# A hybrid attention step on one core: mixer B's transposes moved between the high and low parts of mixer A's values

## The chip, the cores and the metric

The kernel runs on one core of a Trainium2 chip. The metric is the device time of one execution, in microseconds (us). A core has five engines that run side by side, each through its own instructions in order: TensorE (PE; its weight loads are shown apart, as PEld), VectorE (DVE), ScalarE (ACT), GpSimd (POOL) and SyncE (SP, which here issues most of the DMA transfers). A product on TensorE has a stationary operand (the weights, loaded before the pass) and a moving one that streams past it; results land in PSUM, a memory of eight banks, from which the other engines read.

## The reference

One step of a diffusion backbone for 1024 latent tokens and 128 prompt tokens of width 1024, all in float32. A modulated RMSNorm is projected into queries, keys, values and gates of two mixers with 8 heads and 2 key heads each; both mixers attend, are gated, and are projected out together. Cut to what matters here:

```python
p = h @ w_in
q_a, k_a, v_a, g_a, q_b, k_b, v_b, g_b = split(p)     # keys and queries are normalised, turned by position
# mixer A: softmax over 128 context keys and all 1024 latent keys
s = einsum(q_a, k_all) * d ** -0.5 ;  o_a = einsum(softmax(s), v_all)
# mixer B: softmax over a sink column, 128 context keys and a band of 3 x 128 latent keys
s = concat([sink, s_ctx, s_band]) ;   o_b = einsum(softmax(s)[1:], v)
y = x + gate * (concat([o_a * silu(g_a), o_b * silu(g_b)]) @ w_out)
```

The prompt tokens attend to themselves alone, in both mixers.

## The kernel before

**Precision.** TensorE multiplies in a reduced float32 format. To reach the wanted accuracy, operands are split into a high and a low part, and a product becomes three: high by high, high by low, low by high.

**Stages.** First come the projections, up to about 304 us; the rest is attention with the output projection woven in. The attention is cut into *units* (t, m, g): a block t of 128 tokens, a mixer m (0 is A, 1 is B) and a key head g with its four query heads. The order is t = 1 to 8, g, m, so that A and B alternate, and four units of the prompt (t = 0) come last. A unit is cut into blocks of 128 keys, one for each *slot*: 9 slots for a unit of A, 4 for one of B (3 for t = 1 and t = 8), and for a prompt unit one with an empty one behind it. A pair of an A and a B unit so has 13 slots, or 12.

**A slot** is written out by the loop at the end of `hybrid_step`, and the order in which it issues work is kept on every engine (`in_order`). It goes through these steps:

- `tick()` runs what was put on an agenda with `later(n, f)`, n slots before.
- `scores()` of this slot's block. For mixer A: two products give the scores in a PSUM bank (L1190, and L1191 with the queries' low part and the negated row maximum as further rows, tile qb); ScalarE takes the exponential (L1193) and the high part ph (L1194); GpSimd, or VectorE for one block, the low part pl (L1198, L1196). For mixer B: the weights already exist (penat, tile pen), queries by keys, and four 128 x 128 transposes (L1185) turn a block; ScalarE copies the high part ph (L1186), VectorE takes the low part pl one slot later (L1187).
- what is `due` in this slot: row maxima of the A unit to come, and the scores of the B unit to come.
- products of the output projection (L1279), from a queue at OUTRATE in each slot, with the remainder carried over.
- `values()` of the block three slots back (LAG = 3): high values by ph (L1208), for mixer A also low values by ph (L1210, v_lo, 64 columns), high values by pl (L1211). All blocks of a unit add up in one bank.

**Row maxima** (`max_items`): an A unit has twelve, each a product of 384 columns (L918, pmx) and a reduction on VectorE (L919). MX_AT gives their slots, counted from the start of the A unit before (negative ones lie in the pair before that). At MX_END the second copy of the queries is loaded by SP's queue, and VectorE takes the maximum over them (m_nat); TURN slots later TensorE turns it (L937, ptm) and VectorE writes it into qb (L938).

**Mixer B's weights** (`weight_items`): in the first four slots of the A unit before it, a pair of products per head gives scores (L975, L976, tile sn); VectorE masks them and takes the row maximum (L979), ScalarE the exponential one slot later (L965). Then the sinks: a sum on GpSimd, the exponential on ScalarE (EX_AT[0] slots later), the total on GpSimd (EX_AT[1]), the reciprocal on VectorE (L1014, EX_AT[2]). The reciprocals are turned by TensorE (L1027, pti), copied by ScalarE (L1031) and go through DRAM to become rows, which multiply the gate. A prompt unit takes another way: one row maximum over all heads (L991), and VectorE scales the weights themselves (L1017).

**The end of a unit**, in slots counted from its last block by END_AT (PROMPT_END for the prompt): the inverse of the sums on ScalarE (L1222, L1223), the gating (two instructions on VectorE, L1232, and one on GpSimd, L1234), the split into parts, and the products for the output projection put on the queue.

**Banks.** Row maxima, sn, ptm and pti share two banks (A); scores and B's transposes two (B); values two (C); the projection's sums one each (D, E).

Of the kernel before, what the change touches and what calls it, by code (L numbers as in the profile page):

```python
# [9 lines left out]
F32 = mybir.dt.float32  # L10
# [3 lines left out]
ALU = mybir.AluOpType  # L14
# [4 lines left out]
P = 128  # L19
# [17 lines left out]
LAG = 3  # L37
# [4 lines left out]

NAT_AT = (0, 1, 2, 3)
NAT_FIRST = (0, 1, 2, 3)
MX_AT = (-4, -3, -2, -2, -1, 4, 5, 5, 7, 7, 8, 8)
MX_FIRST = (0, 1, 2, 3, 4, 4, 5, 5, 6, 7, 7, 8)
MX_END = 10
SPLIT_LAG = 2

LATE = (5, 5, 5, 5, 4)  # L50
# [3 lines left out]
WO_LATE = {12: 9, 13: 10, 11: 21, 15: 23, 14: 24}  # L54

WO_STEPS = ((0, 4, 4), (1, 5, 5), (2, 6), (3, 7), (4, 8, 6), (5, 9), (6, 11), (7, 12, 10), (8, 12), (9, 13), (10, 14))
TURN = 2
QUERY_AT = (0, 2, 3, 6)
PAD = 2
X_FROM = 2  # L60
# [7 lines left out]
BEHIND = ((), (), (), (), (0,), (1, 2), (3,), (4, 5), (6,), (7,))  # L68
WIDE = 5
LOADLEAD = 5  # L70
OUTRATE = 2.5
PADRATE = 3
POOL_LO = ("gb",)
NOG = 5
PES = 3
GATE_LATE = 2
END_AT = (1, 4, 6, 9)
PROMPT_END = (2, 4, 5, 7)
QTS = 5
PROMPT_LEAD = 4  # L80
EX_AT = (2, 2, 5)
ROWS_AT = (1, 1, 4, 6)
KV_ORDER = [0] + list(range(1, NT))
GATE_AT = (3, 7)
# [33 lines left out]
def hybrid_step(ctx, tc, x_prompt, x_sample, cache_k_a, cache_v_a, cache_k_b, cache_v_b,  # L118
# [3 lines left out]
    nc = tc.nc  # L122
# [13 lines left out]
    def later(n, f):  # L136

        agenda.setdefault(now[0] + n, []).append(f)
# [26 lines left out]
    ident_r = cst.tile([P, P], F32R, name="ident_r")  # L165
# [724 lines left out]
    penat = {}  # L890
# [10 lines left out]
    def max_items(i):  # L901
# [42 lines left out]
                out.append(lambda h=h, b=b: item(h, b))  # L944
        return out, finish

    def weight_items(i):

        t, m, g = units[i]
        v = {}  # L950

        def small(name):
            return qs.tile([P, 4], F32, tag=name, name=f"{name}{i}")

        def first(n):
            if t:
                penat[i] = qp2[0].tile([P, 4, 512], F32, tag="pen", name=f"pen{i}")[:, :, 0:n]
            else:
                penat[i] = w3.tile([P, 512], F32, tag="pe", name=f"pen{i}", bufs=PES).rearrange(
                    "p (h n) -> p h n", h=4)  # L960
            for x in ("nm", "sum", "ex", "inv"):
                v[x] = small(x)

        def exp(h, s, scale):
            nc.scalar.activation(penat[i][:, h], s, AF.Exp, bias=v["nm"][:, h : h + 1], scale=scale,  # L965
                                 accum_out=v["sum"][:, h : h + 1])

        def item(h):
            p0, p1_ = window(t)
            n = P * (p1_ - p0)  # L970
            if h == 0:
                first(n)
            lhs = qtile[i][:, P * h : P * h + P]
            s = bank("A", f"sn{i}_{h}")[:, 0:n]
            nc.tensor.matmul(s, lhs, khb[:, g, p0:p1_, :], start=True, stop=False)  # L975
            nc.tensor.matmul(s, lhs, klb[:, g, p0:p1_, :], start=False, stop=True)  # L976
            m0 = P if t == 1 else 0

            nc.vector.tensor_tensor_reduce(s, s, mask[:, m0 : m0 + n], -1.0, nsink[:, 4 * g + h : 4 * g + h + 1],  # L979
                                           op0=ALU.add, op1=ALU.min, accum_out=v["nm"][:, h : h + 1])  # L980
            later(1, lambda: exp(h, s, -1.0))

        def prompt():
            first(P)
            s = bank("A", f"sn{i}")
            for h in range(4):
                hs = slice(P * h, P * h + P)
                nc.tensor.matmul(s[:, hs], qtile[i][:, hs], khp[:, 2 + g, :], start=True, stop=False)
                nc.tensor.matmul(s[:, hs], qtile[i][:, hs], klp[:, 2 + g, :], start=False, stop=True)
            mx = small("mx4")  # L990
            nc.vector.tensor_reduce(mx, s.rearrange("p (h n) -> p h n", h=4), axis=AX.X, op=ALU.max)  # L991
            nc.vector.scalar_tensor_tensor(v["nm"], mx, -1.0, nsink[:, 4 * g : 4 * g + 4], op0=ALU.mult, op1=ALU.min)
            for h in range(4):
                exp(h, s[:, P * h : P * h + P], 1.0)

        def finish():
            nc.gpsimd.tensor_tensor(v["ex"], v["nm"], sink[:, 4 * g : 4 * g + 4], op=ALU.add)
            if t:
                later(EX_AT[0], sinks)
                later(EX_AT[1], total)  # L1000
                later(EX_AT[2], divide)
            else:
                sinks()
                later(1, total)
                later(1, divide)

        def sinks():
            nc.scalar.activation(v["ex"], v["ex"], AF.Exp)

        def total():  # L1010
            nc.gpsimd.tensor_tensor(v["sum"], v["sum"], v["ex"], op=ALU.add)

        def divide():
            nc.vector.reciprocal(v["inv"], v["sum"])  # L1014
            if t == 0:
                for h in range(4):
                    nc.vector.tensor_scalar(penat[i][:, h], penat[i][:, h], v["inv"][:, h : h + 1], None, op0=ALU.mult)  # L1017
                return

            later(ROWS_AT[0], turned)  # L1020
            later(ROWS_AT[1], put)
            later(ROWS_AT[2], rows)
            later(ROWS_AT[3], lambda: nc.gpsimd.tensor_tensor(sgl[i], sgl[i], v["rows"], op=ALU.mult))

        def turned():
            v["pt"] = bank("A", f"pti{i}")[0:4, 0:P]
            nc.tensor.transpose(v["pt"], v["inv"], ident_r.bitcast(F32))  # L1027

        def put():
            iv = spare[0][0:4, 512 : 512 + P]  # L1030
            nc.scalar.copy(iv, v["pt"])  # L1031
            nc.sync.dma_start(r_dram[i // 2], iv)

        def rows():
            v["rows"] = spare[0][:, 512:768].rearrange("p (c n) -> p c n", c=2)
            for s in range(2):
                nc.sync.dma_start(v["rows"][HD * s : HD * s + HD],
                                  r_dram[i // 2].rearrange("(c s) n -> s c n", s=2)[s : s + 1].to_broadcast([HD, 2, P]))

        return ([lambda h=h: item(h) for h in range(4)] if t else [prompt]), finish  # L1040
# [125 lines left out]
    def load_gate(i):  # L1166
        if i < NU:
            t, m, g = units[i]
            sgl[i] = w2.tile([P, 2, P], F32, tag="sgl", name=f"sgl{i}")
            h0 = HD * (8 * m + 4 * g)  # L1170
            nc.sync.dma_start(
                sgl[i], g_dram[h0 : h0 + 4 * HD, P * place(t) : P * place(t) + P].rearrange("(c p) n -> p c n", p=P))
# [4 lines left out]
    def scores(i, b, blk):  # L1177

        t, m, g = units[i]
        s = bank("B", f"st{i}_{b}")  # L1180
        ph, pl = parts_tiles(i, b)
        if m == 1:
            o = P * blk[0]
            for h in range(4):
                nc.tensor.transpose(s[:, P * h : P * h + P], penat[i][:, h, o : o + P], ident_r.bitcast(F32))  # L1185
            nc.scalar.copy(ph, s)  # L1186
            later(1, lambda: nc.vector.tensor_tensor(pl, s, ph, op=ALU.subtract))  # L1187
            return ph, pl
        kh, kl = blk[0]
        nc.tensor.matmul(s, kh, qtile[i], start=True, stop=False)  # L1190
        nc.tensor.matmul(s, kl, qbtile[i], start=False, stop=True)  # L1191
        pe = w3.tile([P, 512], F32, tag="pe", name=f"pe{i}_{b}", bufs=PES)
        nc.scalar.activation(pe, s, AF.Exp)  # L1193
        nc.scalar.copy(ph, pe)  # L1194
        if b in PL_DVE:
            later(1, lambda: nc.vector.tensor_tensor(pl, pe, ph, op=ALU.subtract))  # L1196
        else:
            nc.gpsimd.tensor_tensor(pl, pe, ph, op=ALU.subtract)  # L1198
        return ph, pl

    def values(i, b, last, blk, ph, pl):
        t, m, g = units[i]
# [3 lines left out]
        pv = pvb[i]  # L1206
        two = vh.rearrange("p s d -> p (s d)")
        nc.tensor.matmul(pv, two, ph, start=(b == 0), stop=False)  # L1208
        if m == 0:
            nc.tensor.matmul(pv[0:64, :], vl, ph, start=False, stop=False)  # L1210
        nc.tensor.matmul(pv, two, pl, start=False, stop=last)  # L1211
# [118 lines left out]
    credit, live = 0.0, []  # L1330
    load_gate(0)
    load_gate(1)
    for s in range(len(slots) + LAG + PROMPT_END[3]):
        tick()
        if s < len(slots):
            live.append((slots[s], slots[s] and scores(slots[s][0], slots[s][1], slots[s][3])))
        for n, at in WO_LATE.items():
            if s == at:
                load_wo(n, w2)
                later(3, lambda n=n: split_wo(n))  # L1340
        for f in due.get(s, ()):
            f()
        for _ in range(LATE[s] if s < len(LATE) else 0):
            late_product(late.pop(0))
        rate = OUTRATE if s < len(slots) and slots[s] else PADRATE
        credit = min(credit + rate, 6.0) if outq else 0.0
        while outq and credit >= 1.0:
            outq.pop(0)()
            credit -= 1.0
        if s >= LAG and live:  # L1350
            slot, parts = live.pop(0)
            if slot:
                values(*slot, *parts)
    for f in outq:
        f()
    in_order(tc)
# [62 lines left out]
```

## Time and profile before

| | |
|---|---|
| median of three runs | 714.93 us (714.61 to 715.21) |
| profiled execution | 714.35 us |
| its span (first to last instruction) | 712.1 us |
| TensorE busy | 694.9 us, 98% of the span |
| VectorE, ScalarE, GpSimd busy | 63%, 60%, 47% |
| granted clock of TensorE | 0.999 |
| first scores of the attention | 304.41 us |

In the profile, L12 is line 12 of the kernel. A row of a timeline reads: start, duration (both us), engine, line, operation, output and input tiles, shapes, number of instructions in the row, and in brackets how long the engine was idle before it and what it waited for. A row "min/median/max" gives durations of one instruction in ns. A row of a waits view names the engine and line that waited, then the one that it waited for, then us in total, times, and the longest. Ends of TensorE's passes are modelled, and passes overlap, so the distance between starts says more than the duration. A row of the windows view is a stretch of time, its length, and the busy time and instructions of each engine in it.

### The profile page before, as it was taken

What the parts mean: (1) busy time and instruction counts of PE and PEld (TensorE: products, weight loads), DVE (VectorE), ACT (ScalarE), POOL (GpSimd) and SP (SyncE); (2) the same over time, 40 slices, a digit from 0 to 9 for tenths busy, and PEclk for the clock granted to TensorE, in tenths of its full rate; (3) what the DMA queues carried; (4) which work ended last, traced back from release to release, by engine and by line L of the source; (5) the groups of instructions that cost most, each with busy time, mean ns of one, the idle gap of its engine ahead of it and who ended that gap; (6) DMA issues with size and microseconds to landing.
All of it is one profiled execution on the core that took longest, in us unless ns stands there. A gap on an engine that the chain in (4) does not pass through costs nothing. (4 is left out here: it accounts for less than half of the span.)

```text
span 712.1 us, 10667 instructions
## 1 busy us (share of the span) xinstructions
PE 694.9 (98%) x3534; PEld 558.3 (78%) x3534; DVE 447.8 (63%) x996; ACT 424.9 (60%) x866; POOL 333.9 (47%) x356
## 2 busy tenths in 40 slices
PE   7999999999999999999999999999999999999987
PEld 3688988877778789986788888878887888887865
DVE  3564257866765963736677577667675776675662
ACT  4555412412323543389877877787778777877760
POOL 3466023233212240356757655765575557555651
PEclk9999999999999999999999999999999999999999
DMA  8960283348434115413222122122221221222323
GB/s 343 416 220 37 99 302 75 83 127 265 95 86 135 41 64 194 148 57 101 83 75 82 38 79 70 55 72 75 68 78 34 83 73 46 81 67 75 104 66 119
DMA packets 53158, 78.56 MB, mean 110 GB/s; under 512 B 6568, under 2 KB 25448, under 8 KB 52080
## 3 DMA queue, kind: packets, MB, share of 16 engines
q1 hardware_dynamic: 45072, 66.22, 27.6%
q10 hardware_dynamic: 8032, 11.68, 6.2%
q8 instruction: 28, 0.46, 0.3%
q14 instruction: 26, 0.21, 0.1%
HBM read 58.69 MB, written 19.18 MB: 109 GB/s over the span
## 5 line engine op out<-in xcount | busy, mean ns | idle before, releaser
L1198 POOL TENSOR_TENSOR pl<-pe,ph 128x512 fp32r<-128x512 f32 x130 | 167.8, 1293 | 150.6 <-DVE nm L979 67.5
L919 DVE TENSOR_REDUCE mx<-pmx 128x1 f32<-128x384 f32 x192 | 101.2, 552 | 55.8 <-PE pmx L918 54.3
L1193 ACT ACTIVATE pe<-st 128x512 f32<-128x512 f32 x146 | 87.0, 596 | 27.5 <-PE st L1191 26.5
L1194 ACT CAST ph<-pe 128x512 fp32r<-128x512 f32 x146 | 90.6, 620 | 4.8
L1208 PE MATMUL pv<-ph,v_hi 128*128 128x512 f32 x208 | 82.8, 398 | 1.8 <-DVE spare L1232 1.8
L1211 PE MATMUL pv<-pl,v_hi 128*128 128x512 f32 x208 | 82.3, 396 | 0.0
L183 POOL TENSOR_TENSOR rs_q<-ms_q,mhalf 128x8 f32<-128x8 f32 x18 | 34.8, 1932 | 82.0 <-DVE ms_q L181 82.0
L1279 PE MATMUL po<-wo,ogh 128*128 128x512 f32 x216 | 72.5, 394 | 0.2 <-DVE yt L1286 0.2
L979 DVE CUSTOM_DVE_ANT_0 sn<-sn,mask,nsink 128x512 f32<-128x512 f32 (+1 forms) x64 | 46.4, 725 | 40.7 <-PE sn L976 40.6
L918 PE MATMUL pmx<-kha,qt 128*128 128x384 f32 x192 | 60.9, 363 | 0.5 <-ACT pen L965 0.3
L1190 PE MATMUL st<-qt,kha 128*128 128x512 f32 x144 | 57.9, 402 | 1.0 <-ACT pe L1193 0.9
L1191 PE MATMUL st<-qb,kla 68*128 68x512 f32 x144 | 57.5, 399 | 1.0 <-DVE qb L938 1.0
L1210 PE MATMUL pv<-ph,v_lo 128*64 128x512 f32 x146 | 57.6, 395 | 0.0
L1211 PEld LDWEIGHTS pv<-pl,v_hi 128*128 128x128 f32 x208 | 39.2, 188 | 16.5
L965 ACT ACTIVATE pen<-sn,nm 128x512 f32<-128x512 f32 (+2 forms) x72 | 45.0, 627 | 5.9 <-DVE nm L979 2.5
L1186 ACT CAST ph<-st 128x512 fp32r<-128x512 f32 x62 | 36.4, 587 | 19.0 <-PE st L1185 17.5
L1208 PEld LDWEIGHTS pv<-ph,v_hi 128*128 128x128 f32 x208 | 39.3, 189 | 10.1 <-ACT ogh L1244 2.4
L1279 PEld LDWEIGHTS po<-wo,ogh 128*128 128x128 f32 x216 | 39.9, 188 | 6.9 <-DVE yt L1286 0.6
L1187 DVE TENSOR_TENSOR pl<-st,ph 128x512 fp32r<-128x512 f32 x62 | 42.5, 685 | 2.1 <-ACT ph L1186 1.5
L1279 PE MATMUL po<-wo,ogl 128*128 128x512 f32 x108 | 42.5, 393 | 0.0
L648 ACT ACTIVATE sqq<-pq 128x512 f32<-128x512 f32 x18 | 10.8, 599 | 51.5 <-DMA qd<-qo0q 16.1
L918 PEld LDWEIGHTS pmx<-kha,qt 128*128 128x128 f32 x192 | 35.5, 190 | 6.5 <-DVE mx L919 1.2
(238 smaller groups left out, 1699.4 us busy)
## 6 DMA issues: line engine op xcount, KB each, us to landing
qt<-qd SPq DMA_DIRECT2D x36, 256.0 KB, 3.0
wm<-in_w_mod_ss_dram SPq DMA_DIRECT2D x8, 1024.0 KB, 12.2
qd<-qo0q ACTq DMA_DIRECT2D x36, 128.0 KB, 2.4
qd<-qo1q ACTq DMA_DIRECT2D x36, 128.0 KB, 2.4
sgl<-gd SPq DMA_DIRECT2D x36, 128.0 KB, 2.4
out_dram<-yt SPq DMA_DIRECT2D x17, 256.0 KB, 2.0
xn<-in_x_sample_dram SPq DMA_DIRECT2D x8, 512.0 KB, 8.2
wg<-in_w_mod_g_dram SPq DMA_DIRECT2D x4, 1024.0 KB, 7.8
```

The lines of the kernel that those rows point to most:

```text
L918: nc.tensor.matmul(pm[:, 0:384], lhs, kha[:, g, 3 * b : 3 * b + 3, :], start=True, stop=True)
L919: nc.vector.tensor_reduce(mx[:, h, b : b + 1], pm[:, 0:384], axis=AX.X, op=ALU.max)
L979: nc.vector.tensor_tensor_reduce(s, s, mask[:, m0 : m0 + n], -1.0, nsink[:, 4 * g + h : 4 * g + h + 1], op0=ALU.add, op1=ALU.min, accum_ou ...
L1190: nc.tensor.matmul(s, kh, qtile[i], start=True, stop=False)
L1191: nc.tensor.matmul(s, kl, qbtile[i], start=False, stop=True)
L1193: nc.scalar.activation(pe, s, AF.Exp)
L1194: nc.scalar.copy(ph, pe)
L1198: nc.gpsimd.tensor_tensor(pl, pe, ph, op=ALU.subtract)
L1208: nc.tensor.matmul(pv, two, ph, start=(b == 0), stop=False)
L1210: nc.tensor.matmul(pv[0:64, :], vl, ph, start=False, stop=False)
L1211: nc.tensor.matmul(pv, two, pl, start=False, stop=last)
L1279: nc.tensor.matmul(po[n], a, wo_parts[KT * n + k][lo], start=(k == KS[0] and p == 0), stop=(k == KS[-1] and p == 2))
```

## The change

The number of instructions stays the same. Mixer B's transposes are no longer issued by `scores()`: it puts them on a list, `turns`, together with the copies that follow them, and `turn_all()` issues what is on the list. `values()` calls it behind its first product. Where the values of a slot belong to mixer A and a block of B is to be turned, the values now come first in the slot, so that TensorE sees: high values by ph, the four transposes, v_lo by ph, high values by pl, then what is due, then the projection. This holds for the first three blocks of each B unit; the fourth, and the prompt's, have no values of mixer A in their slot, and are issued alone where they were. The reciprocals' transpose pti goes behind the group of its slot (`ends_turn`), and its copy behind the group's copy (`after_turn`).

The constants that change with it:

- MX_AT: of the two row maxima in slot -2 one moves to -1, and the one of -1 to 0, the first slot of the next pair.
- MX_END 10 to 9 and TURN 2 to 3: the queries' load and the maximum over the row maxima one slot earlier, ptm in the same slot.
- OUTRATE 2.5 to 2.8: more products of the projection in each slot while the queue lasts.
- END_AT: the gating 3 instead of 4 slots behind a unit's last block.
- EX_AT: the sinks' total one slot behind their exponential, no longer in the same slot.

```diff
-MX_AT = (-4, -3, -2, -2, -1, 4, 5, 5, 7, 7, 8, 8)
+MX_AT = (-4, -3, -2, -1, 0, 4, 5, 5, 7, 7, 8, 8)
-MX_END = 10
+MX_END = 9
-TURN = 2
+TURN = 3
-OUTRATE = 2.5
+OUTRATE = 2.8
-END_AT = (1, 4, 6, 9)
+END_AT = (1, 3, 6, 9)
-EX_AT = (2, 2, 5)
+EX_AT = (2, 3, 5)
...
+    turns, ends_turn, after_turn = [], [], []
+
+    def turn_all():
+        after = [g for _, g in turns]
+        for f, _ in turns:
+            f()
+        for f in ends_turn:
+            f()
+        turns.clear()
+        ends_turn.clear()
+        for g in after + after_turn:
+            g()
+        after_turn.clear()
...
-            later(ROWS_AT[0], turned)
-            later(ROWS_AT[1], put)
+            later(ROWS_AT[0], lambda: ends_turn.append(turned))
...
+            later(ROWS_AT[1] - ROWS_AT[0], put) if ROWS_AT[1] > ROWS_AT[0] else after_turn.append(put)
...
-            for h in range(4):
-                nc.tensor.transpose(s[:, P * h : P * h + P], penat[i][:, h, o : o + P], ident_r.bitcast(F32))
-            nc.scalar.copy(ph, s)
-            later(1, lambda: nc.vector.tensor_tensor(pl, s, ph, op=ALU.subtract))
+
+            def turn_weights():
+                for h in range(4):
+                    nc.tensor.transpose(s[:, P * h : P * h + P], penat[i][:, h, o : o + P], ident_r.bitcast(F32))
+
+            def parts():
+                nc.scalar.copy(ph, s)
+                later(1, lambda: nc.vector.tensor_tensor(pl, s, ph, op=ALU.subtract))
+
+            turns.append((turn_weights, parts))
             return ph, pl
...
         nc.tensor.matmul(pv, two, ph, start=(b == 0), stop=False)
+        turn_all()
         if m == 0:
...
+        early_values = bool(turns) and s >= LAG and live and live[0][0] and units[live[0][0][0]][1] == 0
+        if early_values:
+            next_values()
+        turn_all()
...
-        if s >= LAG and live:
-            slot, parts = live.pop(0)
-            if slot:
-                values(*slot, *parts)
+        if not early_values:
+            next_values()
+        turn_all()
```

More of the change, by code (lines that the diff above doesn't have):

```diff
@@ L1332, in hybrid_step, with next_values @@
     load_gate(1)
+    def next_values():
+        if s >= LAG and live:
+            slot, parts = live.pop(0)
+            if slot:
+                values(*slot, *parts)
     for s in range(len(slots) + LAG + PROMPT_END[3]):
```

## The prediction

> **What bounds the kernel now.** I read the page first, then the table by windows over the attention part, the waits of TensorE, and the timelines around the places that the change touches.
>
> ```profile
> span 712.1 us, 10667 instructions
> PE 694.9 (98%) x3534; PEld 558.3 (78%) x3534; DVE 447.8 (63%) x996; ACT 424.9 (60%) x866; POOL 333.9 (47%) x356
> ```
> ```profile
> core 0: us, PE busy (x) PEld busy (x) DVE busy (x) ACT busy (x) POOL busy (x), PEclk, DMA share, GB/s
> 304.41:323.00 18.59, 18.59 (x98) 15.43 (x96) 8.25 (x19) 17.72 (x37) 10.51 (x10) 1.00 0.21 65
> 323.00:344.30 21.30, 19.67 (x89) 13.67 (x88) 15.09 (x34) 18.53 (x39) 15.27 (x17) 1.00 0.34 107
> 393.44:608.24 214.80, 214.80 (x1037) 172.70 (x1036) 147.01 (x314) 168.64 (x334) 126.84 (x135) 1.00 0.21 67
> 676.18:712.10 35.92, 29.23 (x132) 22.41 (x130) 16.25 (x39) 13.16 (x32) 12.37 (x18) 0.99 0.28 92
> ```
>
> TensorE is busy 694.9 of 712.1 us, at a granted clock of 1.00. Between 393 and 608 us, nine pairs of units of 23.87 us each, it is busy for the whole 214.80 us: no engine makes it wait there. So in that stretch the time is the sum of TensorE's passes, and a change that keeps its instructions can alter it only through the spacing of neighbours, or by bringing in a new wait. What could be won by better order lies at the two ends, in such waits as these (total in us, times, longest):
>
> ```profile
> PE pv L1208 <- DVE spare L1232: 1.8, 3, 0.9
> PE st L1191 <- DVE qb L938: 1.0, 2, 0.5
> ```
>
> **The change part by part.** The number of instructions is the same on every engine; six things move.
>
> *1. The transposes.* There are 62 groups of four: 16 units of mixer B have one for each of three blocks behind the first pass of mixer A's values (48 groups), 12 a fourth one that stands alone, and the two prompt units one each. The 48 stood between the low pass of one block and the next row maximum; now each stands between the high pass and the v_lo pass of one block. The steady timeline, with starts in the first column, prices the old place:
>
> ```profile
> 458.51 0.60 PE L1185 MATMUL st<-ident_r,pen 128*128 128x128 f32 x4
> 458.86 0.42 PE L918 MATMUL pmx<-kha,qt 128*128 128x384 f32 x1
> 459.12 0.40 PE L1208 MATMUL pv<-ph,v_hi 128*128 128x512 f32 x1
> 459.36 0.40 PE L1210 MATMUL pv<-ph,v_lo 128*64 128x512 f32 x1
> 459.59 0.40 PE L1211 MATMUL pv<-pl,v_hi 128*128 128x512 f32 x1
> ```
>
> From 458.51 to 459.12, four transposes and a row maximum take 0.61 us. Passes of 512 columns follow each other at 0.23 to 0.24 us (459.12, 459.36, 459.59). A row maximum has 384 columns, so 384/512 of 0.23 or 0.17 us; the four transposes then take 0.44, or 0.109 each. The next question is whether this 0.109 is the pass itself or the wait for the next weights, since in the new place the next weights, v_lo's, are only 64 columns wide:
>
> ```profile
> 391.59 0.22 PE L937 MATMUL ptm<-ident_r,m_nat 128*4 128x128 f32 x1
> 391.65 0.60 PE L1185 MATMUL st<-ident_r,pen 128*128 128x128 f32 x4
> ```
> ```profile
> 391.59 0.42 PEld L1185 LDWEIGHTS st<-ident_r,pen 128*128 128x128 f32 x4 [0.15 <-PE pv L1210]
> 391.98 0.19 PEld L918 LDWEIGHTS pmx<-kha,qt 128*128 128x128 f32 x1
> 392.09 0.19 PEld L1279 LDWEIGHTS po<-wo,ogl 128*128 128x128 f32 x1
> ```
>
> Here the first transpose starts 0.06 us after ptm did, though its weights began to load only with ptm (391.59): 128 columns of this kind were in within 0.06 us. So the 0.109 of a transpose is its own pass, and a load of up to 0.109 is hidden behind it. The row maximum's load starts with the fourth transpose (391.98), and the load after it 0.11 later (392.09), when the row maximum has taken over: no more than the pass. A narrower load behind the fourth transpose finds nothing left to shorten. I take 0 for the 48 groups; the bounds are 3 ns each way from the rounding of these sums, 48 x 0.003 = 0.15 us. (The unknown refill inside an accumulation is a rival below.)
>
> The Trainium skill's "TensorE: Matmul & The Clock Gate", section "LDWEIGHTS (loading the stationary operand)", says that a load takes its columns divided by 1.2, in ns: an estimate of 107 for 128 columns and 53 for 64. By that rule a transpose's 109 ns could be its load, and the 54 ns saved would count 48 times, 2.6 us; the trace disagrees for the transposes' own weights, which came in within 0.06 us.
>
> Copies on ScalarE and the low parts on VectorE follow the transposes about half a slot later. In the steady stretch ScalarE is busy 168.64 and VectorE 147.01 of 214.80. A slot is 23.87/13 = 1.84 us, and a block is used three slots after its scores (LAG), 5.5 us; half a slot less, 4.6, covers a copy (0.57 in a row of part 5) and a low part one slot after it. Price 0.
>
> *2. Row maxima one slot later, OUTRATE 2.5 to 2.8.* Both only move matmuls within TensorE's full order. Cover for the moved reduction on VectorE: its 32% of idle time. The tight place is slot 0, where a row maximum and a third projection matmul now stand between sn_0 and sn_1:
>
> ```profile
> 465.79 0.40 PE L976 MATMUL sn<-klb,qt 128*128 128x512 f32 x1
> 467.40 0.40 PE L975 MATMUL sn<-khb,qt 128*128 128x512 f32 x1
> ```
> ```profile
> 466.23 0.76 DVE L979 CUSTOM_DVE_ANT_0 sn<-sn,mask,nsink 128x512 f32<-128x512 f32 x1 [0.24 <-PE sn L976]
> ```
> ```profile
> L919 DVE TENSOR_REDUCE mx<-pmx x192: 541/551/559, 277.5 to 648.8; 128x1 f32<-128x384 f32 x192
> ```
>
> sn_1 needs the bank of that row maximum. Its reduction (0.55) stands behind sn_0's masking, which ends at about 467.0 (466.23 + 0.76); so it ends at about 467.6. sn_1, at 467.40 before, comes 0.17 + 0.23 later, at 467.80. The margin is 0.2 us: no wait, price 0.
>
> *3. MX_END 9, TURN 3.* The queries' second transfer on SP's queue and VectorE's maximum go one slot earlier; SP's queue issues 267 instructions in all and is not behind any wait of TensorE in the list above. ptm stays in slot 12, but the twelve-slot pairs still have it directly before st_0, so the wait of L1191 for qb (1.0 in two places) stays. Price 0.
>
> *4. EX_AT.* The sinks' sum goes to GpSimd one slot after their exponential, ahead of a reciprocal that is due two slots later still: 0.
>
> *5. END_AT, and the start of the attention.* Gating (L1232, two VectorE instructions, 0.84 us) comes one slot earlier. In the steady stretch it is covered. At 336 us it is not:
>
> ```profile
> 337.39 0.80 PE L918 MATMUL pmx<-kha,qt 128*128 128x384 f32 x2
> 338.39 0.44 PE L918 MATMUL pmx<-kha,qt 128*128 128x384 f32 x1 [0.20 <-DVE mx L919]
> 338.67 0.40 PE L1208 MATMUL pv<-ph,v_hi 128*128 128x512 f32 x1
> ```
> ```profile
> 334.26 0.69 DVE L1196 TENSOR_TENSOR pl<-pe,ph 128x512 fp32r<-128x512 f32 x1 [2.60 <-ACT ph L1194]
> 335.80 0.84 DVE L1232 TENSOR_TENSOR spare<-pv,rs 64x256 f32<-64x256 f32 x2
> 336.67 2.76 DVE L919 TENSOR_REDUCE mx<-pmx 128x1 f32<-128x384 f32 x5
> ```
>
> Three row maxima take 1.28 us from 337.39 to 338.67 instead of 3 x 0.17: 0.77 lost, as VectorE works off five reductions behind the gating. The gating now falls into the 2.60 us in which VectorE sat idle before 334.26, so the reductions come 0.84 earlier. But three in one slot on two banks still wait for the first one's reduction: an estimate of 0.5 of the 0.55 of L919. Gain 0.77 - 0.5 = 0.27, and 0.17 for the row maximum that has left this stretch. Against it: ScalarE sets the pace here, and receives its copies later.
>
> ```profile
> 321.64 0.60 PE L1185 MATMUL st<-ident_r,pen 128*128 128x128 f32 x4
> 322.34 0.57 ACT L1186 CAST ph<-st 128x512 fp32r<-128x512 f32 x1
> 323.45 0.60 ACT L1222 ACTIVATE rs<-pv 64x512 f32<-64x512 f32 x1
> ```
>
> With the transposes one high pass (0.23) later in each of the first slots, ScalarE's copies slip, and by my following of its queue the inverse of 323.45 begins at 323.82: +0.37. Sum for the start: 0.37 - 0.27 - 0.17 = -0.07; bounds -0.9 (both losses filled, no slip) and +0.4 (the slip alone).
>
> *6. The end.* The prompt units' blocks are alone in their slots. The waits for the gating there:
>
> ```profile
> 682.32 0.48 PE L1208 MATMUL pv<-ph,v_hi 128*128 128x512 f32 x1 [0.16 <-DVE spare L1232]
> 686.06 0.48 PE L1208 MATMUL pv<-ph,v_hi 128*128 128x512 f32 x1 [0.95 <-DVE spare L1232]
> 686.37 0.39 PE L1211 MATMUL pv<-pl,v_hi 128*128 128x512 f32 x1
> ```
> ```profile
> 684.05 0.18 DVE L1014 RECIPROCAL inv<-sum 128x4 f32<-128x4 f32 x1 [1.15 <-POOL sum L1011]
> 684.26 0.88 DVE L1017 TENSOR_SCALAR pen<-pen,inv 128x128 f32<-128x128 f32 x4
> 685.05 0.86 DVE L1232 TENSOR_TENSOR spare<-pv,rs 64x256 f32<-64x256 f32 x2
> ```
>
> The second wait stays: the gating at 685.05 is still queued behind the reciprocal and the scaling (L1017), and these come at the end of the chain of the last prompt unit, which the change starts only 0.06 earlier (ptm no longer ahead of it). What the first wait gives up, the second takes back. Price -0.06, bounds 0 and -1.3 (both waits gone: 0.25 and 1.04, with the 0.09 by which 686.06's pass is longer than 686.37's).
>
> *Sum.* 0 (transposes) + 0 (maxima, projections) + 0 + 0 - 0.07 - 0.06 = -0.13. The profiled execution took 714.35 us, its span 712.1 and 2.25 around it; 0.58 under the median of 714.93. The sum made against it gives 714.2; carried to the median, 714.8.
>
> **The rivals.**
>
> A. *Short load, faster.* The load behind the fourth transpose does cost, and v_lo's is shorter:
>
> ```profile
> L1210 PEld LDWEIGHTS pv<-ph,v_lo x146: 133/134/138, 311.3 to 688.3; 128*64 128x64 f32 x146
> L1208 PEld LDWEIGHTS pv<-ph,v_hi x208: 186/188/192, 311.1 to 689.8; 128*128 128x128 f32 x104
> ```
>
> By these medians 54 ns, 48 times, -2.6 us: 712.3. For it: the loads' widths do show in the rows. Against it: a load within 0.06 us, and 0.11 from load to load, as above. Chance 0.15. (It is the case that the page's rule makes.)
>
> B. *VectorE's waits go, faster.* The gating a slot earlier fills the waits at both ends (-0.9 and up to -1.3) with no slip on ScalarE: 712.7. For it: 2.60 us idle before 334.26. Against it: the chain at 684. Chance 0.13.
>
> C. *A refill in the accumulation, slower.* The values' accumulation is broken by another tile's transposes; if the pass that takes it up again starts like one after an idle TensorE, it costs 0.09 us (0.48 at 686.06 against 0.39 at 686.37), 48 x 0.09 = 4.3: 719.2. It decides from 0.03 a group (1.43 us in all). For it: no row of before shows a transpose inside a values' accumulation. Against it: transposes followed other passes without a gap. Chance 0.11.
>
> D. *The bank at slot 0, slower.* If VectorE comes to the moved reduction later than I follow it, sn_1 waits. Each 0.1 beyond the margin of 0.2 costs 0.1 in 14 pairs; at 0.15, 2.1 us and 717.0. It decides from 0.1. Against it: VectorE is 32% idle. Chance 0.1.
>
> **How the numbers follow.** 0.2% (1.43 us) is about what this measurement can tell from no change. The forecast case, 714.8, has 0.51 with an own range of 713.6 to 715.4, all within 0.2%. A and B end faster (0.28), C and D slower (0.21), nearly all of it beyond 0.2%. The range from 712.3 to 717.2 takes in A, B and D, and leaves out C and half a case's spread below.
>
> **What would show it.** Right: a pair between 393 and 608 us still of 23.87 us; 0.44 from the first transpose to v_lo; no new wait of sn in the list; the wait of L1208 for the gating near 1 us at 686. The time of A would show as 0.38 instead of 0.44 there, and pairs of 23.71; that of C as pairs of 24.1; that of D as sn waiting for mx. I would be wrong most likely by the ends: ScalarE's slip, or a wait that takes the place of one of the three.

## The result, and the profile after

The changed kernel takes 718.59 us (median; 717.9 to 719.53) beside 714.96 for the one before: a ratio of 1.0042, 95% interval 1.0024 to 1.0060. It is slower: by 3.6 us between the medians, by 3.0 by the ratio. The forecast was 714.8, no change, and its range ended at 717.2.

The page and the windows view of the changed kernel (columns as before; the third row holds the nine pairs that took 214.80 before):

```profile
span 715.9 us, 10730 instructions
PE 696.2 (97%) x3534; PEld 560.3 (78%) x3534; DVE 460.3 (64%) x996; ACT 425.4 (59%) x866; POOL 339.8 (47%) x356
```
```profile
304.60:323.60 19.00, 18.70 (x96) 15.49 (x96) 7.35 (x17) 17.31 (x36) 10.51 (x10) 1.00 0.18 52
323.60:345.12 21.52, 19.38 (x87) 13.89 (x88) 15.13 (x34) 18.57 (x40) 15.09 (x16) 1.00 0.34 111
394.66:610.74 216.08, 216.08 (x1037) 173.85 (x1036) 155.51 (x314) 169.45 (x333) 131.35 (x135) 1.00 0.21 66
679.54:715.90 36.36, 29.20 (x132) 22.50 (x130) 17.12 (x40) 13.09 (x32) 12.37 (x18) 0.97 0.27 90
```

Two things stand out. The nine steady pairs take 216.08, or 24.01 each in place of 23.87, with the same 1037 products and no idle time of TensorE that the view sees. And VectorE is busy 12.5 us longer (460.3 against 447.8) with the same 996 instructions. One instruction accounts for most of the second. Its row, of the kernel before and then of the changed one (shortest, median and longest, in ns):

```profile
L932 DVE TENSOR_SCALAR m_nat<-m x16: 170/419/836, 288.4 to 651.1; 128x4 fp32r<-128x4 f32 x16
```
```profile
L932 DVE TENSOR_SCALAR m_nat<-m x16: 169/1264/1270, 288.7 to 652.4; 128x4 fp32r<-128x4 f32 x16
```

L932 negates four numbers in each partition; alone it takes 0.17 us. It is the instruction that MX_END moves. Here is one pair of the changed kernel: VectorE and GpSimd, then TensorE in the third slot of the transposes.

```profile
436.83 1.26 DVE L932 TENSOR_SCALAR m_nat<-m 128x4 fp32r<-128x4 f32 x1
438.00 0.55 DVE L919 TENSOR_REDUCE mx<-pmx 128x1 f32<-128x384 f32 x1
438.47 0.67 DVE L1206 TENSOR_TENSOR pl<-st,ph 128x512 fp32r<-128x512 f32 x1
```
```profile
436.78 1.28 POOL L1219 TENSOR_TENSOR pl<-pe,ph 128x512 fp32r<-128x512 f32 x1 [0.27 <-ACT ph L1215]
```
```profile
438.96 0.40 PE L1229 MATMUL pv<-ph,v_hi 128*128 128x512 f32 x1
439.29 0.63 PE L1202 MATMUL st<-ident_r,pen 128*128 128x128 f32 x4
439.68 0.47 PE L1232 MATMUL pv<-ph,v_lo 128*64 128x512 f32 x1
```

GpSimd's subtraction runs from 436.78 to 438.06. L932 begins within it, at 436.83, and ends at 438.09, right behind it. What is queued behind it on VectorE comes late: the low part of the first block of mixer B (L1206) ends at 439.14. The third group of transposes writes the bank that this low part reads, so it starts at 439.29, 0.15 behind that end and 0.33 behind the high pass, where a pass takes 0.23. In the kernel before, in the same place of the pair:

```profile
460.39 0.15 DVE L929 TENSOR_REDUCE m<-mx 128x4 f32<-128x12 f32 x1
460.58 0.42 DVE L932 TENSOR_SCALAR m_nat<-m 128x4 fp32r<-128x4 f32 x1
```
```profile
458.99 1.29 POOL L1198 TENSOR_TENSOR pl<-pe,ph 128x512 fp32r<-128x512 f32 x1 [0.69 <-ACT ph L1194]
460.24 0.74 POOL L1246 TENSOR_TENSOR ogl<-spare,ogh 128x256 fp32r<-128x256 f32 x1
```

There L932 came when GpSimd's shorter product (460.24 to 460.98) had 0.4 left, and ended at 461.00; the reduction L929, beside the same product, took its plain 0.15. So a hold was in the trace of before too, at 0.42 in place of 0.17.

By the starts of the first scores of each pair, the 3.8 us between the two profiled spans lie as follows: 0.2 up to the first scores; +0.42, +0.22 and +0.22 in the first three pairs; +1.60 in the next eleven (from 23.84 to 23.87 each to 23.99 to 24.04); +0.16 and +0.57 in the last two; +0.45 from the prompt's first scores to TensorE's last pass ("prompt and tail" below: 30.80 before, 31.25 changed). The waits of TensorE that are new in the list belong to the two ends:

```profile
PE pv L1229 <- DVE spare L1254: 2.2, 2, 1.5
PE pmx L915 <- DVE qb L938: 0.4, 1, 0.4
PE sn L990 <- DVE qb L938: 0.3, 1, 0.3
```

### The profile page after: what moved, and what is told of

It is laid out like the page before. It is cut to its first block, busy times and chain, and to the rows that moved or that the text cites. A ratio compares the mean times of both kernels' runs of the same rounds, so it can differ in the third digit from the quotient of the medians.

```text
span 715.9 us, 10730 instructions
## 1 busy us (share of the span) xinstructions
PE 696.2 (97%) x3534; PEld 560.3 (78%) x3534; DVE 460.3 (64%) x996; ACT 425.4 (59%) x866; POOL 339.8 (47%) x356
## 5 line engine op out<-in xcount | busy, mean ns | idle before, releaser
L1232 PE MATMUL pv<-ph,v_lo 128*64 128x512 f32 x146 | 61.5, 421 | 0.0
L1206 DVE TENSOR_TENSOR pl<-st,ph 128x512 fp32r<-128x512 f32 x62 | 42.3, 682 | 2.1 <-ACT ph L1205 1.6
```

## The experiments

The theory was formed from these rows, and the expectations call it L: GpSimd holds L932, VectorE's queue slips, and a bank of the scores comes free late; TURN 3 costs one wait for a bank in the first unit and one in the prompt. The rival, R, is that breaking the accumulation (the prediction's C), or the moved reductions, cost the 0.15 of a pair.

**1. MX_END and TURN put back in the changed kernel**

```diff
-MX_END = 9
+MX_END = 10
-TURN = 3
+TURN = 2
```

> The changed kernel with MX_END back at 10 and TURN back at 2, all else changed. Theory L (the small VectorE instruction L932, moved by MX_END to where GpSimd starts its 1.29 us subtraction, is held until that ends and makes the low part, and with it the third group of transposes, late; TURN = 3 costs one bank wait in the first unit and one in the prompt): L932 takes about 0.42 us, a pair in the steady stretch takes 23.85 to 23.90 us as before, sn no longer waits for qb near 307 us (0.53), nor pmx for qb in the prompt (0.6); 13 x 0.15 + 0.53 + 0.6 = 3.1 less than the change: about 715.5. Rival R (breaking the accumulation, or the moved reductions, cost the 0.13 to 0.16 per pair): pairs stay at 24.0, only the 1.1 of the two ends goes: about 717.4.

Measured: 716.88 us, ratio to before 1.0030 (1.0018 to 1.0042). L932 takes 0.17 in all steady pairs, and the nine take 214.96, 23.88 each: L, and not R. The time fell by 1.7 and not by 3.1, since a wait that nobody had before appears in the two pairs that follow twelve slots, and the profiled run (717.87, 1.0 above the median) also lost 1.4 us up to the first scores, of which the last section tells:

```profile
PE st L1212 <- DMA qb<-qd: 2.6, 2, 1.5
```

In the new order the transfer of qb, one slot later, lands too late there.

**2. MX_END and TURN alone, in the kernel before**

```diff
-MX_END = 10
+MX_END = 9
-TURN = 2
+TURN = 3
```

> The kernel before with MX_END 9 and TURN 3 alone. Theory L: L932 lands in GpSimd's subtraction here too (about 1.2 us), but the third group of transposes stood 0.77 us behind the low part that it needs, and keeps its place at the head of the slot: pairs of 23.87 to 23.95. The two bank waits of TURN come (0.5 + 0.6): about 716.1. If the hold alone costs the pair its 0.15 whatever the place of the transposes: pairs of 24.0 and about 718. Rival R: pairs of 23.87, and L932 at 0.42 or less.

Measured: 720.36 us, 1.0080 (1.0065 to 1.0095), and pairs of 24.13 to 24.43. I had expected 716.1 and missed it: L932 is held here as foreseen (0.94 to 1.25), but what suffers is not the low part. The reduction behind L932 comes late, and with it the bank of the next row maximum.

**3. All constants new, the transposes in their old place**

> The kernel before with all the new constants, the transposes in their old place. Theory L: as with MX_END and TURN alone, pairs of 23.87 to 23.95, two waits of TURN, about 716. If the constants alone carry the whole loss: pairs of 24.0, 718 to 718.6. Rival R in the form that breaking the accumulation costs: pairs of 23.87.

Measured: 723.04 us, 1.0113 (1.0098 to 1.0128), pairs of 24.44. The same mechanism, in one pair of this kernel:

```profile
462.35 1.28 POOL L1198 TENSOR_TENSOR pl<-pe,ph 128x512 fp32r<-128x512 f32 x1 [0.27 <-ACT ph L1194]
462.40 1.26 DVE L932 TENSOR_SCALAR m_nat<-m 128x4 fp32r<-128x4 f32 x1
463.57 0.55 DVE L919 TENSOR_REDUCE mx<-pmx 128x1 f32<-128x384 f32 x1
464.17 0.46 PE L918 MATMUL pmx<-kha,qt 128*128 128x384 f32 x1 [0.34 <-DVE mx L919]
```

So the constants alone cost 8.2 us and the new place gives 4.5 of them back: in it the row maxima stand behind the values, some 0.7 us later, and the late bank no longer stops them.

**4. The place alone, all constants old**

```diff
-MX_AT = (-4, -3, -2, -1, 0, 4, 5, 5, 7, 7, 8, 8)
-MX_END = 9
-TURN = 3
-OUTRATE = 2.8
-END_AT = (1, 3, 6, 9)
-EX_AT = (2, 3, 5)
+MX_AT = (-4, -3, -2, -2, -1, 4, 5, 5, 7, 7, 8, 8)
+MX_END = 10
+TURN = 2
+OUTRATE = 2.5
+END_AT = (1, 4, 6, 9)
+EX_AT = (2, 2, 5)
```

> The new place of the transposes with all the old constants. Theory L says that the place itself costs nothing: pairs of 23.87 to 23.90 in the steady stretch. Against it stand, from the run with MX_END 10 and TURN 2, waits of two twelve-slot pairs for the queries' second transfer (+0.5 and +0.85 on these pairs): about 716.2 to 716.5. The tail keeps its old length, as the gating is where it was. If the place costs by itself (a refill, or a low part that comes late), pairs of 24.0 and 718.

Measured: 721.22 us, 1.0102 (1.0078 to 1.0126), pairs of 24.20. Again my figure was wrong, by a wait that I hadn't named, and not by the place as such. The two row maxima of slot -2 now end their slot, and ptm opens the next one and needs the bank of the first:

```profile
465.69 1.02 DVE L919 TENSOR_REDUCE mx<-pmx 128x1 f32<-128x384 f32 x2 [0.17 <-PE pmx L918]
```
```profile
465.67 0.61 PE L1301 MATMUL po<-wo,ogh 128*128 128x512 f32 x2
466.30 0.23 PE L937 MATMUL ptm<-ident_r,m_nat 128*4 128x128 f32 x1
```

ptm starts 0.41 behind the second product (which began at 465.89) where 0.23 is usual, in every pair, and the transposes and the row maximum behind it take 0.06 longer. Neither the place nor the constants can be judged alone: each breaks a fit that the other keeps.

**5. The negation on ScalarE, all else as changed**

```diff
-            nc.vector.tensor_scalar(mn, m4, -1.0, None, op0=ALU.mult)
+            nc.scalar.activation(mn, m4, AF.Copy, scale=-1.0)
```

> The changed kernel with the negation L932 as one ScalarE instruction in place of VectorE's, in the same slot. Theory L: nothing holds VectorE in that slot, the wait of the third group goes, pairs of 23.85 to 23.90; the two waits of TURN stay: 718.6 - 1.9 = about 716.7. Rival R: pairs stay at 24.0, about 718.6.

Measured: 716.77 us, 1.0025 (1.0015 to 1.0034), as expected by L. The nine pairs, by the windows view:

```profile
395.47:610.42 214.95, 214.95 (x1037) 174.61 (x1036) 145.13 (x305) 170.40 (x342) 131.32 (x135) 1.00 0.21 67
```

They lose 1.13 against the changed kernel, and summed over equal neighbours all of it lies in two kinds of step: from a high pass to the transposes (0.88 in 27 places) and between transposes (0.25). VectorE's work in the stretch falls by 10.4 us. Against the kernel before, 0.15 is left in the nine pairs, or 5.6 ns for each of their 27 groups if all of it is put down to them. How much of it is the new place itself isn't shown, as the moved row maxima and projection products and the negation on ScalarE are in it too.

**6. The same, with TURN 2 for the first two units of mixer A and the prompt**

```diff
-            later(TURN, transpose)
+            later(2 if t == 0 or i in EARLY else TURN, transpose)
```

> The changed kernel with the negation on ScalarE, and TURN 2 for the two first units of mixer A and for the prompt alone. Theory L: beside the steady stretch's 1.8 also the waits of sn (0.53 near 307 us) and of the prompt's pmx (0.6) for qb go: 718.6 - 1.8 - 1.1 = about 715.7. If these two waits are only passed on to a later one: 716.8, as with the negation on ScalarE alone.

Measured: 717.1 us, 1.0033 (1.0019 to 1.0047). The first pair is back at 18.55 (19.01 before this edit), the last one at 23.04 (23.68); yet the time did not fall, as the prompt and the tail take 32.04 in place of 31.25. The edit of experiment 5 now costs its own wait there, at 681.53: ScalarE does the negation behind its other work when ptm needs it at once (the first row; the second lies at 290.90, ahead of the attention, and is a wait for a row maximum):

```profile
PE ptm L937 <- ACT m_nat L932: 0.9, 1, 0.9
PE ptm L937 <- DVE mx L919: 0.8, 1, 0.8
```

**7. The gating back at 4**, on top of 6, and then (12) in the changed kernel alone

```diff
-END_AT = (1, 3, 6, 9)
+END_AT = (1, 4, 6, 9)
```

> The same, with END_AT back at 4 for the gating. In the prompt, the changed kernel has the row maximum's L1007 held for 0.55 by a GpSimd product that the earlier gating pushed 0.7 later. Theory L: with the gating at 4, L1007 takes 0.16 again and the wait of the last gating is 0.55 shorter: 715.1, or 0.2 off the kernel before. If the tail's loss comes from the order of the projection instead: 715.7, and L1007 still 0.7 or the wait as long.

> The changed kernel with the gating back at END_AT 4, and nothing else. The run with END_AT 3 on the kernel before showed L992 held (0.72 in place of 0.16) and a tail 0.5 longer. Theory L: here L1007 takes 0.16 again, the wait of 1.67 for the last gating falls by 0.55, and the steady pairs fall or stay as the other GpSimd work moves: 718.0 or less. If END_AT 3 was needed by the new order: 719 or more.

Measured: 716.62 us (1.0027, 1.0016 to 1.0037) on top of 6; 716.40 (1.0021, 1.0012 to 1.0031) alone, 2.2 less than the changed kernel. On top of 6 I had expected 715.1 and missed it: L1007 takes 0.16 again, but ptm still waits 0.93 for ScalarE in the prompt, and prompt and tail stay at 31.93. With the gating alone put back, the second pair is back at 21.28, prompt and tail at 30.75, and the held L932 costs 0.07 in a pair, not 0.15: the hold now lasts 0.06 less (1.21). L1007 takes 0.16 here too. From the first scores on, the profiled execution is 1.6 shorter than that of the changed kernel; the rest of the 2.2 isn't seen in these two traces.

**8. The gating at 3 in the kernel before**

> The kernel before with the gating at END_AT 3 alone. The prediction had it gain at the start (up to 0.27) and nothing at the end: 714.7. Theory L: it moves GpSimd's product into the prompt's L1007 (0.7 in place of 0.16) and costs 0.5 at the end, so 715.2 to 715.5; the steady pairs stay at 23.87.

Measured: 715.72 us, 1.0010 (0.9999 to 1.0021), which by itself doesn't tell it from the kernel before. In the trace all pairs are as before, and the tail is 0.53 longer. The same hold, on another instruction, in the chain on which the last gating waits:

```profile
681.77 0.74 POOL L1023 TENSOR_TENSOR sgl<-sgl,spare 128x256 f32<-128x256 f32 x1
```
```profile
681.81 0.72 DVE L992 SCALAR_TENSOR_TENSOR nm<-mx,nsink 128x4 f32<-128x4 f32 x1
```

L992 takes 0.16 in the kernel before. The earlier gating put another GpSimd product ahead of L1023, and so L1023 on top of L992.

**9. The negation inside the reduction, TURN and END_AT as in 7**

```diff
-                nc.vector.tensor_reduce(m4, mx, axis=AX.X, op=ALU.max)
+                nc.vector.tensor_reduce(mn, mx, axis=AX.X, op=ALU.max, negate=True)
             else:
-                m4 = mx[:, :, 0]
-            nc.vector.tensor_scalar(mn, m4, -1.0, None, op0=ALU.mult)
+                nc.vector.tensor_scalar(mn, mx[:, :, 0], -1.0, None, op0=ALU.mult)
```

> The changed kernel with the negation done inside VectorE's reduction over the twelve maxima (L932 is gone but for the prompt, no instruction on ScalarE), TURN 2 for the first two units of mixer A and the prompt, and the gating at END_AT 4. Theory L: a reduction that starts within GpSimd's subtraction isn't held (0.16), pairs of 23.88; ptm no longer waits for ScalarE as it did with the negation there (0.9 near 290 us, 1.09 in the prompt); nothing else is left of the change's loss: 714.7 to 715.2, no difference from before. If the new order costs something that none of the named waits explains: 716.0 or more. If the reduction is held like L932: pairs of 24.0.

Measured: 716.32 us, 1.0023 (1.0014 to 1.0033). Here I was wrong: 1.2 us of the change's loss stay. No wait of ptm is left near 290 us, and the first two pairs are as before (18.55, 21.30). But the steady pairs take 23.95, with up to 4 ns more in many kinds of step and no place where it gathers. Some of it isn't of the new order: in the kernel before, the same negation (experiment 10) goes with pairs of 23.85 to 23.92, against 23.87 without it (11). And the prompt and the tail take 31.77 in place of 30.80. Here the hold is back: L1005, the L992 of the kernel before, takes 0.53 and not 0.16, and ends with GpSimd's product.

```profile
682.42 0.53 DVE L1005 SCALAR_TENSOR_TENSOR nm<-mx,nsink 128x4 f32<-128x4 f32 x1
```
```profile
682.20 0.74 POOL L1035 TENSOR_TENSOR sgl<-sgl,spare 128x256 f32<-128x256 f32 x1
```

With 0.19 by which ptm comes later, its 0.37 make the reciprocal of the last prompt unit 0.56 later, counted from the prompt's first scores. Of the rest, 0.35 lies in the last 14 us, where the same passes as before stand further apart. Why the spacings widen is open.

**10 and 11. The kernel before, with MX_END one slot earlier after the two pairs of twelve slots**, where ptm stood directly before st_0; with the negation inside the reduction, and without

```diff
-start[i - 2] + MX_END
+min(start[i - 2] + MX_END, start[i] - 3)
```

> The kernel before with the negation inside the reduction, and with MX_END one slot earlier for the two units that follow a pair of twelve slots, where ptm stood directly before st_0 and L1191 waited 0.70 for qb. Both pairs lose that wait and its restart, 2 x 0.8: 713.3, faster than both kernels. If another wait takes its place (the queries' transfer comes too late as it did with MX_END 10 in the new order, or a bank): 714.9.

> The kernel before with MX_END one slot earlier after the two pairs of twelve slots, the negation left as it was. Beside the kernel that also has the negation inside the reduction (713.8): if the gain is that of qb alone, 713.4 to 713.8 again; if L932, now in slot 9 of these two pairs, is held by GpSimd's subtraction for 1.2 us, the two pairs lose part of it: 714.0 to 714.5.

Measured: 713.78 us, 0.9985 (0.9976 to 0.9994), with the negation inside the reduction; 713.17 us, 0.9977 (0.9967 to 0.9987), without. Both are faster than both kernels. The wait of L1191 for qb is gone, and nothing took its place. The first row is of the kernel before, the other two of the run without the negation inside:

```profile
345.23 0.50 PE L1191 MATMUL st<-qb,kla 68*128 68x512 f32 x1 [0.50 <-DVE qb L938]
```
```profile
344.39 0.47 PE L1190 MATMUL st<-qt,kha 128*128 128x512 f32 x1
344.69 0.39 PE L1191 MATMUL st<-qb,kla 68*128 68x512 f32 x1
```

The two pairs take 24.57 and 22.36 in place of 25.30 and 23.13. L932 is held in one of the two places (1.20), where nothing waits for it. That the negation inside the reduction gains nothing here fits: no wait of the kernel before names L932.

## Why the prediction was wrong

**The step that failed is part 3**, "MX_END 9, TURN 3 ... Price 0". I followed the moved work through SP's queue and TensorE's waits, and gave the instruction L932 no place in time on VectorE. It already took 0.42 and not 0.17 in the trace of before. In its new slot it takes 1.26, the low part of the first block comes late, and the third group of transposes waits: 1.13 in nine pairs, taken away by experiment 5 with one instruction moved and by experiment 1 with the slot put back. TURN 3 in the same part costs the first pair 0.46 and the last one 0.64, which experiment 6 takes back. (SP's queue issues 292 transfers in the trace of before, not 267; nothing hangs on it.)

**Part 1, the passes, held; two of its readings did not, and its "Price 0" for the copies had less margin than it reckoned.** In experiment 5, whose third group isn't late, a group and v_lo's pass take 0.67 (439.82 to 440.49 below); less 0.23 for the pass, the group takes 0.44, as in the old place. So v_lo's narrow load gains next to nothing, and rival A is out. But the sign named for it, 0.44 from the first transpose to v_lo, was wrong: the next pass starts 0.35 behind the first transpose in the old place (458.51 to 458.86) and in the new one (439.82 to 440.17), and the rest of the 0.44 shows behind that pass. Nor do the rows show that a transpose's weights were in within 0.06: that is the distance of two starts, while the load's own row lasts 0.14:

```profile
L1185 PEld LDWEIGHTS st<-ident_r,pen x248: 138/141/144, 318.5 to 686.8; 128*128 128x128 f32 x124
```

"Price 0" for ScalarE's and VectorE's following was worked out for the products that use the blocks, three slots on. The bank that the low part frees is needed two slots on, by the third group. Without the hold, in experiment 5, the low part ends at 439.52 and the group starts at 439.82, as these rows of VectorE and TensorE show. Of these 0.3 us, 0.15 is the distance that stayed when the group did wait (439.14 to 439.29); so the margin was about 0.15.

```profile
438.84 0.68 DVE L1206 TENSOR_TENSOR pl<-st,ph 128x512 fp32r<-128x512 f32 x1
```
```profile
439.82 0.60 PE L1202 MATMUL st<-ident_r,pen 128*128 128x128 f32 x4
440.17 0.48 PE L1232 MATMUL pv<-ph,v_lo 128*64 128x512 f32 x1
440.49 0.40 PE L1233 MATMUL pv<-pl,v_hi 128*128 128x512 f32 x1
```

**Part 5, the gating, failed in sign:** END_AT 3 was to gain up to 0.27 at the start. In the changed kernel it costs 0.24 in the second pair (experiment 12); in the kernel before it changes nothing there (experiment 8).

**Part 6, the end, failed:** I saw that the last gating's chain sets the end, and priced it at -0.06 by what the change does to TensorE's order. That the earlier gating reorders GpSimd, and that GpSimd holds a link of this chain (L992), I didn't see: it costs 0.53 in experiment 8, and 12 takes 0.50 back.

**Part 2 held, in the changed kernel:** sn_1's margin at slot 0 was enough; no wait of sn stands in the steady pairs. Experiment 4 shows what its constants are for.

**The rivals:** C, a refill in the accumulation, is out: in experiment 5 the broken accumulation stays and the loss of the pairs goes. D had the right kind, VectorE late and a bank with it, and the wrong place, slot 0 in place of slot 11; it had no cause for the lateness, and so too small a chance. The total, 718.6, lies 1.4 beyond the range because three losses came together: the held L932, TURN 3 and the gating. Taken back all at once, in experiment 9, they give 2.3 of the 3.6 us; why 1.2 stay is open but for what is said there.

## What to carry to other kernels

When a small VectorE instruction is moved, ask what GpSimd runs at the moment where it lands; compare its duration in the trace with its shortest one, and price the move by the rest of GpSimd's instruction, for everything queued behind. Check the reuse of each bank as well as the use of each result. Where an order is tuned, its constants are fitted to each other: one alone, put back or carried over, may cost more than all together (here 5.5, 6.4 and 8.2 us against 3.6).

## What the runs showed of the hardware

**GpSimd holds some of VectorE's instructions until its own has ended.** L932 ends 0.02 to 0.03 us behind GpSimd's instruction in every steady pair of both kernels, and takes 0.42 or 1.26 by where in it it began (0.93 to 1.25 in experiment 2). The Trainium skill says so in "SBUF — State Buffer", section "Who interferes with whom": the two engines share a pair of ports, whoever issues first keeps it for the whole instruction, and tensor_scalar can take it, as can an instruction with two inputs in SBUF, while a reduction doesn't on this chip. The trace agrees: L932 is a tensor_scalar; L992, held for 0.72, has two such inputs; the reduction L929 took 0.15 beside GpSimd's product at 460.39.

**Which of the two comes first can differ between two executions with the same order of work.** Near 285 us both engines have a subtraction for the output projection's weights to do. In the kernel before, VectorE comes first; in experiment 1, where TensorE, VectorE, ScalarE and GpSimd have had the same order up to there, GpSimd does. The rows of VectorE and GpSimd, of the one and of the other:

```profile
285.45 0.68 DVE L1075 TENSOR_TENSOR wo<-wraw,wo 128x512 fp32r<-128x512 f32 x1
285.48 1.81 POOL L1075 TENSOR_TENSOR wo<-wraw,wo 128x512 fp32r<-128x512 f32 x1 [1.25 <-ACT wo L1074]
```
```profile
285.79 1.65 DVE L1090 TENSOR_TENSOR wo<-wraw,wo 128x512 fp32r<-128x512 f32 x1
285.60 1.29 POOL L1090 TENSOR_TENSOR wo<-wraw,wo 128x512 fp32r<-128x512 f32 x1 [0.96 <-ACT wo L1089]
```

The one that comes second takes longer by what is left of the other. In experiment 1 the row maxima behind it on VectorE came late, and the first scores at 305.78 in place of 304.41. Not all of that is the tie: experiment 1 was 0.4 later already at 282 us, and in experiment 2, where GpSimd also came first, the first scores stand at 304.93. Whether this is also why executions of one kernel differ, by up to 3.7 us in experiment 9, was not tried.
